# Encoder with two mixers: the last layer's second MLP product in three sweeps of seven block products, with weight sums made in DRAM

## The chip, the core and the metric

The kernel runs on one core of one Trainium2 chip. The core has five engines that run side by side and meet at semaphores: TensorE (PE; its weight loads are listed as PEld), VectorE (DVE), ScalarE (ACT), GpSimd (POOL) and SyncE (SP), which only starts transfers. ScalarE and GpSimd can start transfers too; 16 DMA engines carry them out. Each engine takes its instructions in the order of its queue. The time is the device time of one execution in microseconds; lower is better.

## The reference: what is computed

Two layers over 512 tokens (a grid of 8 x 64) of width 1024, all in float32. Layer 0 mixes with grouped-query attention and latent attention side by side, layer 1 with attention over a neighbourhood. Behind each stands an MLP with a squared ReLU, of hidden width 4096, and at the end an RMS norm.

```python
def sq_relu_mlp(h, w_up, w_down):
    u = jax.nn.relu(h @ w_up)
    return (u * u) @ w_down
...
        h = h + sq_relu_mlp(rmsnorm(h, norm_ffn[layer]), ffn_w_up[layer], ffn_w_down[layer])
    return rmsnorm(h, final_norm)
```

## The kernel before

The residual stays in SBUF as `hT`, features on partitions, 8 tiles of 128 features by 512 tokens. Every factor is split into a high part (written as float32r by ScalarE, `whi`) and a remainder (by VectorE, `wlo`), and every product is three matmuls: high by high, high by remainder, remainder by high. Weights come through a list of planned chunks: `plan` notes a chunk, `weights(i)` starts loads up to five chunks ahead and conversions two ahead. Large tiles are 30 slots of 128 x 1024 (`Slot`).

**The opening.** x and the first 768 columns of `w_in` are loaded in pieces by SP. For each of 8 feature tiles TensorE transposes x (`make_x`, L540), ScalarE and VectorE split it (L544, L545), and six output tiles are summed (`use_w`, L501 to L503). ScalarE squares each tile (`sumsq_acc`, L515) and POOL adds the squares up (L517) into `acc`; TensorE turns `acc` into row norms (`compact_r`, L522). Then come the statistics of key and queries (`stat`): ScalarE squares, VectorE rounds (L594), POOL makes the remainder (L595), TensorE sums both (L596, L597). The rotary products are POOL's too (L562, L563). `q_scales` gives the factor by which the scores of the first attention are scaled (L1001).

**The first attention** (`attend`) goes through 16 heads in four steps each, `step` being called once per step to run other products in between (`fill`).

**The MLPs** (`mlp(l)`). The first product makes hidden tiles, in groups (`SIZES`); most of it uses `Seven`, a scheme with seven instead of eight products of half-size blocks, whose weight sums POOL makes (`seven_chunk`, L302 to L304) and whose matmuls have 256 columns (L388 to L390). The second product for layer 1 takes 6, 8 and 6 of the 32 hidden tiles in plain form (`product`, matmuls of 512 columns), then 8 tiles in the `Seven` form, for which `convert` makes token sums and splits (L336 to L340, L362, L363), and the last 4 tiles with tokens on partitions (`last`, `down`), where the result meets the transposed residual (`turn`), the final norm and the output's transfers. `evac` (L1295) and `ev` (L1265) add to `hT`.

**What sets the order.** Outside the second attention (`fixed_order`) a scheduler places the instructions: it lets an engine take any instruction whose inputs are there, with the program's order as a preference, not as a rule. A transfer that depends on nothing can thus stand far ahead of its place in the text. Transfers share a small number of semaphores in turn, so that a new transfer may have to wait until an older one with the same semaphore has landed.

Of the kernel before, what the change touches and what calls it, by code (L numbers as in the profile page):

```python
# [8 lines left out]
F32 = mybir.dt.float32  # L9
# [26 lines left out]
def encoder_kernel(ctx: ExitStack, tc: tile.TileContext, ins, out, dbg=None):  # L36
# [736 lines left out]
    rope_q(0)  # L773


    kst = Slot()

    def ev_kr(b):
# [316 lines left out]
    attend(all_heads(), step)  # L1095
    fill.until("out")
    ok = [s_.pair() for s_ in O[4:]]
    flip[0] = 1
# [11 lines left out]
    def first_product(l):  # L1110

        w = ins["ffn_w_up"][l]
        X = [Slot() for _ in range(KD)]
        acc = pp.tile([P, S], F32, tag="p", name=nm("acc"))
        for k in range(KD):
            split_g(hT[:, k, :], gffn(l, k), X[k].pair())
            sumsq_acc(k, acc, DVE)
        xp = [s_.pair() for s_ in X]
        U, R = [], []
        rb = keep([P, S], F32, "rb")  # L1120
        state = dict(c=SIZES[l][0], ids=None, plain=False, split=iter(()))
# [24 lines left out]

        def raw_evac(w_):
            ACT.activation(w_.t, w_.t, AF.Relu)
            ACT.activation(w_.t, w_.t, AF.Square)
            R.append(w_)  # L1150
            return True

        def pair_evac(w_):
            raw_evac(w_)
            R.pop()
            for z in range(2):
                U.append(Slot())
                split(w_.t[:, S * z : S * z + S], U[-1].pair())

        def plain():  # L1160
            four = product(w, 0, xp, tiles(0, 512), ev, lambda n: [mmb(), mmb(), mmb(), sbk()])
            two = product(w, 0, xp, tiles(512, 256), ev, lambda n: [sbk(), ob()], kstep=4)
            for n, _ in enumerate(four):
                if n == (11 if l == 0 else 13):
                    norm()
                if n == 14:
                    x_sums(0)
                    x_sums(1)
            for n, _ in enumerate(two):
# [20 lines left out]
        def stage(n, raw=0, more=0):  # L1190

            if not state["plain"]:
                plain()
            left = n + raw + more - len(U)
            while left:
                i = state["ids"]
                state["c"] += 2
                left -= 2
                if left:
                    ahead()  # L1200
                for _ in x7.run(i, raw_evac if more <= left < more + raw else pair_evac):
# [12 lines left out]

    def bias_rows():
        R, Fi, Fe = Slot(F32), Slot(F32), Slot(F32)
        rpb = ins["od_rpb"][0]
        for qr in range(8):
            SP.dma_start(R.t[16 * qr : 16 * qr + 16, 0:248],
                           rpb.rearrange("h a b -> h (a b)")[:, (7 - qr) * 31 : (7 - qr) * 31 + 248])  # L1220
            yield
        POOL.memset(Fi.t[:, 0:376], NEG)
        POOL.memset(Fe.t[:, 256:512], NEG)
        rv = R.t[:, 0:248].rearrange("p (k d) -> p d k", d=31)
        POOL.tensor_copy(Fi.t[:, 0:376].rearrange("p (j k) -> p j k", k=8)[:, 15:31, :], rv[:, 7:23, :])
        POOL.tensor_copy(Fe.t[:, 0:248].rearrange("p (j k) -> p j k", k=8), rv)
        for _ in range(6):
            yield
        bxv = bx.rearrange("h t (c r) k -> t c r h k", r=8)
        for c in range(16):  # L1230
            SP.dma_start(bxv[0, c].rearrange("r h k -> r h k"), Fi.t[:, (15 - c) * 8 : (15 - c) * 8 + 256])
            yield

            v, off = (1, (7 - c) * 8) if c < 8 else (0, (23 - c) * 8)
            SP.dma_start(bxv[1, c][:, :, 128 * v : 128 * v + 128], Fe.t[:, off : off + 128])
            yield
            SP.dma_start(bxv[1, c][:, :, 128 - 128 * v : 256 - 128 * v], Fe.t[:, 256:384])
            yield
        for s_ in (R, Fi, Fe):
            s_.free()  # L1240
        yield

    def convert(u7, R):
        held = tc.keep_in_program_order
# [332 lines left out]
    def last_mlp():  # L1577
# [43 lines left out]
        def down(k0, c, up, tail):  # L1621

            nk = len(up)
            ids = [plan([(0, S, rows(ins["ffn_w_down"][1], k0 + k, 2)[:, :, S * c : S * c + S])], 2, S)
                   for k in range(0, nk, 2)]

            def run():
                banks = group(4)

                def use(k, j):  # L1630
                    wh, wl = (x[:, k % 2, :] for x in weights(ids[k // 2]))
                    uh, ul = (up[k][:, z, j * P : (j + 1) * P] for z in range(2))
# [22 lines left out]
        def last(k0, tiles_):  # L1655
# [4 lines left out]
            def beside(m, i):  # L1660
                if m == 2 and i == 0:
# [3 lines left out]
                if m > 1 and i in (16, 22):  # L1665
                    turn(2 * (m - 2) + (i == 22), 0)
# [62 lines left out]
```

## Time and profile before

| | us |
|---|---|
| median of 3 runs (1182.7 to 1184.34) | 1183.78 |
| the profiled execution: span | 1184.0 |
| first matmul of a score (L997) | 68.95 |
| row norms' matmuls (L522): first attention | 40.6 |
| the same, first MLP | 276.4 |
| the same, second attention | 613.3 |
| the same, last MLP | 838.1 |

The norms' matmuls mark the stages: what is called the opening here are the first 69 us, the last MLP is what runs from about 838 us to the end. A row of the windows gives a stretch's length, the busy time of PE, PEld, DVE, ACT and POOL with counts, TensorE's granted clock, the share of the 16 DMA engines and GB/s. A row of the timeline gives start, duration, engine, line, operation, result and inputs, and in brackets how long the engine had been idle and who ended that. A row of the waits gives who waited for whom: total, times, longest.

### The profile page before, as it was taken

What the parts mean: (1) busy time and instruction counts of PE and PEld (TensorE: products, weight loads), DVE (VectorE), ACT (ScalarE), POOL (GpSimd) and SP (SyncE); (2) the same over time, 40 slices, a digit from 0 to 9 for tenths busy, and PEclk for the clock granted to TensorE, in tenths of its full rate; (3) what the DMA queues carried; (4) which work ended last, traced back from release to release, by engine and by line L of the source; (5) the groups of instructions that cost most, each with busy time, mean ns of one, the idle gap of its engine ahead of it and who ended that gap; (6) DMA issues with size and microseconds to landing.
All of it is one profiled execution on the core that took longest, in us unless ns stands there. A gap on an engine that the chain in (4) does not pass through costs nothing.

```text
span 1184.0 us, 19784 instructions
## 1 busy us (share of the span) xinstructions
PE 1160.5 (98%) x7128; PEld 1021.2 (86%) x7128; DVE 883.2 (75%) x1514; ACT 640.3 (54%) x1081; POOL 526.1 (44%) x662
## 2 busy tenths in 40 slices
PE   9989999999999999999999999999999999999997
PEld 8667778888899899988998998988889989998895
DVE  5788998878967368786884676667996736778975
ACT  4468676664546247562553565555554624666344
POOL 3267343224562377819602232231376625774710
PEclk9999999999999999999999999999999999999998
DMA  7223225212524723225226464433352341322412
GB/s 244 71 54 92 68 78 134 62 56 77 167 86 134 263 70 90 72 90 165 67 72 178 131 184 126 116 112 109 107 165 76 115 134 55 98 64 89 143 36 71
DMA packets 110145, 128.01 MB, mean 108 GB/s; under 512 B 9075, under 2 KB 86816, under 8 KB 110048
## 3 DMA queue, kind: packets, MB, share of 16 engines
q1 hardware_dynamic: 106992, 119.30, 33.5%
q0 software_dynamic: 2304, 6.31, 2.2%
q8 instruction: 56, 0.92, 0.3%
q10 hardware_dynamic: 752, 1.15, 0.3%
q14 instruction: 41, 0.34, 0.1%
HBM read 104.32 MB, written 6.29 MB: 93 GB/s over the span
## 4 chain that ended last, share of the span: by engine, by line
PE 81%; DVE 4%; ACT 1%; issue 1%; POOL 0%; DVEq 0%; ACTq 0%
PE mm L503 8%; PE mm L501 8%; PE mm L502 8%; PE mm L390 4%; PE mm L389 4%; PE mm L388 4%; PE t L388 3%; PE t L389 3%; PE t L390 3%; PE s L502 2%; PE s L503 2%; PE s L501 2%; PE s L390 2%; PE s L388 2%; PE s L389 2%; PE s L997 2%
## 5 line engine op out<-in xcount | busy, mean ns | idle before, releaser
L309 DVE TENSOR_TENSOR wlo<-a,whi 128x896 fp32r<-128x896 f32 x132 | 161.8, 1230 | 83.7 <-ACT whi L308 82.9
L308 ACT ACTIVATE whi<-a 128x896 fp32r<-128x896 f32 x132 | 125.0, 950 | 155.0 <-PE o L502 45.8
L501 PE MATMUL mm<-a,whi 128*128 128x512 f32 x485 | 195.9, 406 | 0.9 <-DVE a L915 0.7
L503 PE MATMUL mm<-a,wlo 128*128 128x512 f32 x485 | 192.1, 397 | 2.5 <-DVE wlo L202 2.5
L502 PE MATMUL mm<-a,whi 128*128 128x512 f32 x485 | 192.5, 397 | 0.1
L202 DVE TENSOR_TENSOR wlo<-raw,whi 128x1024 fp32r<-128x1024 f32 (+4 forms) x117 | 139.3, 1193 | 66.4 <-ACT whi L212 63.9
L212 ACT ACTIVATE whi<-raw 128x1024 fp32r<-128x1024 f32 (+3 forms) x120 | 116.4, 971 | 92.2 <-PE s L502 39.8
L302 POOL TENSOR_TENSOR a<-a 128x128 f32<-128x128 f32 x132 | 85.1, 645 | 173.3 <-DMA a<-in_ffn_w_up_dram 103.9
L303 POOL TENSOR_TENSOR a<-a 128x256 f32<-128x256 f32 x132 | 120.2, 910 | 10.3
L304 POOL TENSOR_TENSOR a<-a 128x128 f32<-128x128 f32 x132 | 115.1, 872 | 10.3
L503 PEld LDWEIGHTS mm<-a,wlo 128*128 128x128 f32 x485 | 91.7, 189 | 23.7 <-DVE wlo L202 3.4
L501 PEld LDWEIGHTS mm<-a,whi 128*128 128x128 f32 x485 | 91.8, 189 | 20.4 <-PE t L972 0.9
L502 PEld LDWEIGHTS mm<-a,whi 128*128 128x128 f32 x485 | 91.9, 190 | 17.4 <-DVE a L545 0.4
L388 PE MATMUL mm<-a,whi 128*128 128x256 f32 x370 | 103.9, 281 | 0.0
L389 PE MATMUL mm<-a,whi 128*128 128x256 f32 x370 | 103.9, 281 | 0.0
L390 PE MATMUL mm<-a,wlo 128*128 128x256 f32 x370 | 103.7, 280 | 0.0
L1005 POOL TENSOR_SCALAR p<-p,ti 128x512 f32<-128x512 f32 x64 | 46.2, 724 | 92.3 <-DVE ti L1004 81.1
L1430 POOL TENSOR_SCALAR p<-p,ti 128x256 f32<-128x256 f32 x64 | 35.6, 567 | 104.8 <-DVE ti L1429 91.8
L388 PE MATMUL t<-a,whi 128*128 128x256 f32 x264 | 74.2, 281 | 0.0
L389 PE MATMUL t<-a,whi 128*128 128x256 f32 x264 | 74.1, 281 | 0.0
L390 PE MATMUL t<-a,wlo 128*128 128x256 f32 x264 | 73.9, 280 | 0.0
L390 PEld LDWEIGHTS mm<-a,wlo 128*128 128x128 f32 x370 | 69.6, 188 | 0.2 <-DVE wlo L309 0.2
(338 smaller groups left out, 3210.8 us busy)
## 6 DMA issues: line engine op xcount, KB each, us to landing
a<-in_ffn_w_up_dram SPq DMA_DIRECT2D x104, 256.0 KB
raw<-in_ffn_w_down_dram SPq DMA_DIRECT2D x46, 512.0 KB
raw<-in_od_w_qkv_dram SPq DMA_DIRECT2D x64, 128.0 KB
a<-in_ffn_w_down_dram SPq DMA_DIRECT2D x28, 256.0 KB
raw<-in_ffn_w_up_dram SPq DMA_DIRECT2D x12, 512.0 KB
raw<-in_ev_w_in_dram SPq DMA_DIRECT2D x12, 384.0 KB
a<-a SPq DMA_DIRECT2D x18, 256.0 KB
bias<-bx SPq DMA_DIRECT2D x16, 256.0 KB
```

The costliest lines, as they stand in the source:

```text
L202: z = lambda: (eng or DVE).tensor_tensor(to, src, f32(high), op=ALU.subtract)
L212: ACT.activation(hi[:, 0:m], raw[:, 0:m], AF.Copy)
L303: POOL.tensor_tensor(r[:, 4:6], r[:, 2:3].to_broadcast([P, 2, P]), r[:, 0:7:6], op=ALU.add)
L304: POOL.tensor_tensor(r[:, 7], r[:, 3], r[:, 5], op=ALU.subtract)
L308: ACT.activation(hi[:, 0:896], raw[:, 128:1024], AF.Copy)
L309: DVE.tensor_tensor(lo[:, 0:896], raw[:, 128:1024], f32(hi[:, 0:896]), op=ALU.subtract)
L388: PE.matmul(o, wh, x[:, 0], start=kp == 0 and n in (0, 1, 3, 5), stop=False, skip_group_check=True)
L389: PE.matmul(o, wh, x[:, 1], start=False, stop=False, skip_group_check=True)
L390: PE.matmul(o, wl, x[:, 0], start=False, stop=kp == self.np - 1, skip_group_check=True)
L501: PE.matmul(o, wh, xh, start=first, stop=False)
L502: PE.matmul(o, wh, xl, start=False, stop=False)
L503: PE.matmul(o, wl, xh, start=False, stop=last)
```

## The change

In layer 1, `mlp_swept` takes the place of `mlp`. Six hidden tiles go through the plain product as before. The next 22 stay in float32 (11 slots `R`, each with two tiles) and the second product over them is made in three sweeps over all 11 pairs (`Sweeps`): two, two and three of the seven block products, each for four output tiles at once, in six PSUM banks. Token sums are made in place on VectorE just ahead of each step and split into a slot. Weight operands are blocks of the weights or sums of blocks, all with plus signs. The sums aren't made on POOL when a chunk is loaded, but once, in DRAM (`SumsAhead`): ScalarE's queue copies the 11 pairs of weight rows (1 MB each) to a DRAM tile `made`, and POOL's queue starts four adding DMAs of 256 KB for each pair. The program asks for one of them in each step of the first attention from the fifth on. The transposes `turn(j, 0)` move into `down`.

```diff
+    class SumsAhead:
+        def __init__(self, w, k0, n):
+            self.w, self.k0, self.n = w, k0, n
+            self.made = dr.tile([n, 2, P, 1024], F32, name=nm("made"))
...
+        def steps(self):
+            for kp in range(self.n + 4):
+                if kp < self.n:
+                    k = self.k0 + 2 * kp
+                    ACT.dma_start(self.made[kp].rearrange("z p c -> (z p) c"), self.w[k * P : (k + 2) * P, :])
+                for back, z, f, src in ((2, 1, 1, lambda q: self.weight(q, 0, 1)), (2, 0, 1, lambda q: self.weight(q, 0, 0)),
+                                        (3, 0, 0, lambda q: self.block(q, 1, 1)), (4, 1, 0, lambda q: self.block(q, 0, 0))):
+                    if 0 <= kp - back < self.n:
+                        POOL.dma_start(self.block(kp - back, z, f), src(kp - back), accum_op=ALU.add)
+                        yield
...
+        if n > 3:
+            next(sums1, None)
         fill.run(1.5)
 
+    ahead1 = SumsAhead(ins["ffn_w_down"][1], FIRST, RAW // 2)
+    sums1 = ahead1.steps()
...
+    def sweep_chunk(w, k0, kind, made):
...
+        if kind == 0:
+            for z in range(2):
+                SP.dma_start(line(a[:, S * z : S * z + S]), half(k0 + z, 0))
+        else:
+            for z in range(2):
+                SP.dma_start(line(a[:, S * z : S * z + S]), blocks(made[z])[:, (z, 1 - z)[kind - 1]])
...
+        ACT.activation(hi, a, AF.Copy)
+        DVE.tensor_tensor(lo, a, f32(hi), op=ALU.subtract)
...
+            if kind == 0:
+                split_to(d[:, :, 0], d[:, :, 1], r[:, 0:4:2])
+                self.one(kp)
+                if kp < 2:
+                    self.two(kp)
+            elif kind == 1:
+                for q, src in enumerate((r[:, 0], s2)):
+                    split_to(d[:, q, 0], d[:, q, 1], src)
+                if kp + 2 < self.n:
+                    self.two(kp + 2)
...
+            PRODUCTS = [
+                [(X, 0, at(0)), (Z, 1, at(S))],
+                [(Y, 0, at(S)), (X, 1, at(0))],
+                [(Y, 2, at(S)), (Z, 1, lambda h, m: (h[2].t[:, 0:S], h[2].t[:, S:], P * m)), (X, 0, at(0))],
+            ]
...
+                PE.matmul(o, wh, x[:, 0], start=first and m % 2 == 0, stop=False, skip_group_check=True)
+                PE.matmul(o, wh, x[:, 1], start=False, stop=False, skip_group_check=True)
+                PE.matmul(o, wl, x[:, 0], start=False, stop=last, skip_group_check=True)
...
+                if c == 0:
+                    for j in range(4):
+                        turn(j, 0)
...
-        mlp(1, last)
+        mlp_swept(1, ahead1, last)
```

Where the new transfers stand in the built program. First POOL's queue at the very start, as a difference (`made` is the DRAM tile, `acc` the sum of squares, `sc` a scratch tile):

```order
 L130 DMA a_82<-in_final_norm_dram 8x128
+L806 DMA made_621<-in_ffn_w_down_dram 256x256 x4
+L806 DMA made_621<-made_621 256x256 x2
+L806 DMA made_621<-in_ffn_w_down_dram 256x256
 L517 ISA
 L517 TENSOR_TENSOR acc_122<-acc_122,sc_248 128x512
+L806 DMA made_621<-in_ffn_w_down_dram 256x256
 L517 TENSOR_TENSOR acc_122<-acc_122,sc_283 128x512
+L806 DMA made_621<-made_621 256x256
```

Seven adding DMAs now stand ahead of POOL's first addition of squares, and more between the next ones. Second, POOL's queue at the remainders of the key's and the first query tile's statistics (L595), with the semaphores each instruction waits for (DMAHW: a transfer from SP or ScalarE; DMASW: one from POOL). Before:

```order
L517 TENSOR_TENSOR acc_122<-acc_122,sc_384 128x512 [waits Activation_49,Pool_49]
L595 TENSOR_TENSOR sc_434<-sc_432,sc_433 128x512 [waits DVE_49]
L562 TENSOR_TENSOR sc_475<-sc_440,a_132 128x512 [waits PE_49,DMAHW7_49,Activation_49,Pool_49]
L595 TENSOR_TENSOR sc_524<-sc_522,sc_523 128x512 [waits DVE_49,PE_49]
L595 TENSOR_TENSOR sc_539<-sc_537,sc_538 128x512 [waits DVE_49,Pool_49]
```

And in the change, the end of that stretch:

```order
L806 DMA made_621<-made_621 256x256 [waits DMASW7_49,DMASW4_49]
L806 DMA made_621<-in_ffn_w_down_dram 256x256 [waits DMAHW6_49]
L806 DMA made_621<-in_ffn_w_down_dram 256x256 [waits DMASW6_49]
L806 DMA made_621<-made_621 256x256 [waits DMASW1_49]
L806 DMA made_621<-made_621 256x256 [waits DMASW3_49,DMASW0_49]
L806 DMA made_621<-made_621 256x256 [waits DMASW5_49]
L595 TENSOR_TENSOR sc_524<-sc_522,sc_523 128x512 [waits DVE_49,PE_49]
```

Ahead of this L595 stand 42 of the 44 adding DMAs (30 of them ahead of the key's L595); the wait for DMAHW6 in the second row is the one for the last of the 11 copies. Third, ScalarE's queue in the opening, in the change (`whi`: weight casts; `a_114`, `a_115`: tiles of x; before, the same casts and tiles stand there without the L802 rows):

```order
L140 ACTIVATE ti_109<-zeros 128x1 [waits Pool_49]
L802 DMA made_621<-in_ffn_w_down_dram 16x16384
L802 DMA made_621<-in_ffn_w_down_dram 16x16384 [waits DMAHW0_49]
L143 ACTIVATE gT<-t_111 128x16 [waits PE_49]
L212 ACTIVATE whi_150<-raw_148 128x768 [waits DMAHW6_49]
L544 ACTIVATE a_114<-t_155,gT 128x512 [waits PE_49,Activation_49]
L544 ACTIVATE a_115<-t_167,gT 128x512 [waits PE_49]
L802 DMA made_621<-in_ffn_w_down_dram 16x16384 [waits DMAHW3_49]
L212 ACTIVATE whi_177<-raw_175 128x768 [waits DMAHW1_49]
```

Two copies are started before the first tile of x is scaled, and all 11 before the seventh (`a_120`).

More of the change, by code (lines that the diff above doesn't have):

```diff
@@ L1095, in encoder_kernel @@
     attend(all_heads(), step)
+    assert next(sums1, 0) == 0
     fill.until("out")
@@ L1120, in first_product @@
         rb = keep([P, S], F32, "rb")
-        state = dict(c=SIZES[l][0], ids=None, plain=False, split=iter(()))
+        state = dict(c=FIRST, ids=None, plain=False, split=iter(()))
         x7 = Seven(KD)
@@ L1188, in ahead, with stage @@
             state["ids"] = x7.plan(w, P * state["c"])
-        def stage(n, raw=0, more=0):
+        def stage(n, raw=0, more=0, then=lambda: None):
             if not state["plain"]:
@@ L1200, in stage @@
                     ahead()
+                else:
+                    then()
                 for _ in x7.run(i, raw_evac if more <= left < more + raw else pair_evac):
@@ L1241, in bias_rows, with raw, half @@
         yield
+    def sweep_chunk(w, k0, kind, made):
+        def raw():
+            slot = Slot(F32) if len(free) > reserve[0] else None
+            return slot, slot.t if slot else wp.tile([P, 1024], F32, tag="raw", bufs=4, name=nm("raw"))
+        def half(k, f):
+            return w[k * P : (k + 1) * P, :].rearrange("p (z f n) -> p f z n", z=2, f=2)[:, f]
+        sa, a = raw()
+        sb, b = raw() if kind == 2 else (None, None)
+        if kind == 0:
+            for z in range(2):
+                SP.dma_start(line(a[:, S * z : S * z + S]), half(k0 + z, 0))
+        else:
+            for z in range(2):
+                SP.dma_start(line(a[:, S * z : S * z + S]), blocks(made[z])[:, (z, 1 - z)[kind - 1]])
+        if kind == 2:
+            SP.dma_start(line(b[:, 0:S]), half(k0 + 1, 1))
+        yield
+        hi = wp.tile([P, 1024], F32R, tag="whi", name=nm("whi"))
+        lo = wp.tile([P, 1024], F32R, tag="wlo", name=nm("wlo"))
+        ACT.activation(hi, a, AF.Copy)
+        DVE.tensor_tensor(lo, a, f32(hi), op=ALU.subtract)
+        third = None
+        if kind == 2:
+            third = Slot()
+            ACT.activation(third.t[:, 0:S], b[:, 0:S], AF.Copy)
+            DVE.tensor_tensor(third.t[:, S:], b[:, 0:S], f32(third.t[:, 0:S]), op=ALU.subtract)
+        for s_ in (sa, sb):
+            if s_:
+                s_.free()
+        yield (hi, lo, third), None, []
@@ new lines, in mlp_swept, with ev, split_more @@
+    def mlp_swept(l, made, last):
+        stage, ahead, later = first_product(l)
+        w = ins["ffn_w_down"][l]
+        U = stage(FIRST)[0]
+        up = [s_.pair() for s_ in U]
+        def ev(m, b):
+            DVE.tensor_tensor(hT[:, m, :], hT[:, m, :], b, op=ALU.add)
+        gens = [product(w, 0, up, tiles(512 * c, 512), lambda j, b, c=c: ev(4 * c + j, b)) for c in range(2)]
+        ahead()
+        for c, gen in enumerate(gens):
+            for i, _ in enumerate(gen):
+                later(c, i)
+        for s_ in U:
+            s_.free()
+        reserve[0] = 3
+        sweeps = []
+        R = stage(0, RAW + MORE, 0, lambda: sweeps.append(Sweeps(w, FIRST, made)))[1]
+        R, more = R[: RAW // 2], R[RAW // 2 :]
+        V = [Slot() for _ in range(MORE)]
+        def split_more():
+            for n, v in enumerate(V):
+                raw = more[n // 2]
+                split(raw.t[:, S * (n % 2) : S * (n % 2) + S], v.pair())
+                if n % 2:
+                    raw.free()
+                yield
+        rest = split_more()
+        reserve[0] = 6
+        beside = last(FIRST + RAW, V)
+        for n, (kind, kp) in enumerate(sweeps[0].run(R)):
+            beside(kind, kp)
+            if n % 16 == 15:
+                next(rest, None)
+        assert next(rest, 0) == 0
+        reserve[0] = 1
@@ L1658, in last, with beside @@
             runs.extend(down(k0, c, up, 2 + 2 * c) for c in range(2))
-            def beside(m, i):
-                if m == 2 and i == 0:
+            def beside(kind, kp):
+                if (kind, kp) == (2, 6) and not H:
                     H.extend(Slot(F32) for _ in range(4))
@@ L1664, in beside @@
                     SP.dma_start(G[0].t, ins["final_norm"].unsqueeze(0).to_broadcast([P, D]))
[L1665 to L1670 removed]
+            return beside
+        mlp_swept(1, ahead1, last)
+        flip[0] = 1
         for run in runs:
```

131 lines of the change are left out of this document (added).

## The prediction

> **What bounds the kernel now.** I read the page's busy table and its slices first, to see whether one engine sets the time.
>
> ```profile
> span 1184.0 us, 19784 instructions
> PE 1160.5 (98%) x7128; PEld 1021.2 (86%) x7128; DVE 883.2 (75%) x1514; ACT 640.3 (54%) x1081; POOL 526.1 (44%) x662
> PE   9989999999999999999999999999999999999997
> PE 81%; DVE 4%; ACT 1%; issue 1%; POOL 0%; DVEq 0%; ACTq 0%
> ```
>
> TensorE is busy for 98% and makes up 81% of the chain that ended last; POOL is nowhere on that chain. So the time is TensorE's work plus its few gaps. The profiled execution's 1184.0 us agrees with the median of the runs, 1183.78 us, and I sum against 1184.0. A difference under 0.2%, about 2.4 us, is what a measurement of this kernel can't tell from no change.
>
> Next, the two places that the change touches. In the last MLP (from about 838 us) the waits of TensorE, and the timeline behind the one that matters:
>
> ```profile
> PE mm L503 <- DVE wlo L202: 2.2, 1, 2.2
> 1102.58 0.79 PE L503 MATMUL mm<-a,wlo 128*128 128x512 f32 x1 [2.23 <-DVE wlo L202]
> 1103.17 0.63 PE L501 MATMUL mm<-a,whi 128*128 128x512 f32 x1
> ...
> 1106.56 0.40 PE L501 MATMUL mm<-a,whi 128*128 128x512 f32 x1
> ```
>
> TensorE waits there once, 2.23 us, while VectorE converts the raw tiles for the old seven-product part. Behind it nine matmuls take 3.39 us instead of nine times 0.232: another 1.3 us.
>
> The opening, by windows (columns: length; busy time of PE, weight load, DVE, ACT and POOL with counts; granted clock; DMA share; GB/s):
>
> ```profile
> 0.00:54.00 54.00, 51.79 (x251) 42.32 (x252) 32.02 (x70) 24.23 (x37) 14.28 (x22) 1.00 0.50 163
> 10.00:15.00 5.00, 5.00 (x26) 4.11 (x25) 3.42 (x6) 3.28 (x5) 1.52 (x1) 1.00 1.07 392
> 45.00:80.00 35.00, 28.56 (x117) 19.78 (x116) 28.56 (x75) 18.30 (x34) 14.32 (x11) 0.95 0.23 62
> ```
>
> TensorE is full nearly from the start, and the transfers of the first 54 us are 163 GB/s x 54 us = 8.8 MB. When the 16 DMA engines are full (share 1.07) they load 392 GB/s, that is 366 GB/s at a share of 1.
>
> POOL's place in the opening, from its timeline:
>
> ```profile
> 30.46 1.29 POOL L517 TENSOR_TENSOR acc<-acc,sc 128x512 f32<-128x512 f32 x1 [3.27 <-ACT sc L515]
> 40.67 1.27 POOL L595 TENSOR_TENSOR sc<-sc,sc 128x512 fp32r<-128x512 f32 x1 [8.92 <-DVE sc L594]
> 53.91 1.29 POOL L595 TENSOR_TENSOR sc<-sc,sc 128x512 fp32r<-128x512 f32 x1 [10.26 <-DVE sc L594]
> PE t L597 <- POOL sc L595: 1.4, 3, 0.8
> ```
>
> POOL idles for its inputs here, but TensorE waits for each of these results: L517's sum feeds the row norms (L522), L595's remainders feed the statistics of key and queries (L597), and without these no score is scaled. POOL's idleness is slack only as long as nothing that waits stands in front of these instructions.
>
> **The MLP, part by part.** Removed: 14 contraction tiles of plain second product, 8 tiles x 14 x 3 = 336 matmuls of 512 columns. Added: they join the seven-product part, so its block products go from 4 x 4 x 7 x 3 = 336 to 11 x 7 x 4 x 3 = 924 matmuls of 256 columns. TensorE's step, start to start, for the two kinds:
>
> ```profile
> 879.69 0.40 PE L501 MATMUL mm<-a,whi 128*128 128x512 f32 x1
> 881.78 0.40 PE L501 MATMUL s<-a,whi 128*128 128x512 f32 x1
> ...
> 1009.81 0.28 PE L390 MATMUL s<-a,wlo 128*128 128x256 f32 x1
> 1011.93 0.28 PE L390 MATMUL s<-a,wlo 128*128 128x256 f32 x1
> ```
>
> Between the first two lie 9 steps: 2.09/9 = 0.232 us. Between the other two lie 18: 2.12/18 = 0.118 us. So 336 x 0.232 = 78.0 us go, 588 x 0.118 = 69.3 us come: **8.7 us less**. The burst of conversions that caused the 2.23 us wait goes as well, since tokens are now converted one step ahead of each sweep step: 2.2 + 1.3 = 3.5 us. What is late next there is VectorE. It now does in each step of a sweep one weight remainder of 1024 columns, token remainders of 512 (768 and a weight remainder of 512 in the third sweep) and one or two sums of 256:
>
> ```profile
> L202 DVE TENSOR_TENSOR wlo<-raw,whi 128x1024 fp32r<-128x1024 f32 x8 | 10.1, 1263 | 7.6 <-ACT whi L212 7.6
> L363 DVE TENSOR_TENSOR a<-a,a 128x512 fp32r<-128x512 f32 x12 | 10.6, 925 | 0.7 <-ACT a L362 0.7
> L363 DVE TENSOR_TENSOR a<-a,a 128x256 fp32r<-128x256 f32 x4 | 1.9, 478 | 0.0
> L1265 DVE TENSOR_TENSOR hT<-hT,mm 128x512 f32<-128x512 f32 x3 | 1.9, 675 | 0.0
> L363 DVE TENSOR_TENSOR a<-a,a x68: 406/684/1231, 308.3 to 1105.0; 128x512 fp32r<-128x512 f32 x51, 128x256 fp32r<-128x256 f32 x17
> ```
>
> The first three rows, means of 1060 to 1150 us, are beside a busy POOL. With them the three sweeps' steps cost 1.26 + 0.93 + 0.48 = 2.67, 1.26 + 2 x 0.48 + 0.48 = 2.70 and 1.26 + 2 x 0.93 + 3 x 0.48 = 4.56 us, against TensorE's 24, 24 and 36 matmuls: 2.83, 2.83 and 4.25 us. Near its limit in the first two, above it in the third. But POOL no longer makes sums in this stage, and L363's median and minimum of one (684 and 406 ns) say what such pieces take undisturbed: 2.3, 2.5 and 3.9 us, below TensorE. I cost the sweeps at TensorE's time; if that cover is gone, eleven steps of the third sweep lose 0.3 us each and the 8 additions into the residual between the sweeps 0.68 us each (L1265): about 9 us. The weights' loads (512 KB in 2.83 us, 185 GB/s) are below the 392 of the window above. The transposes of the first half move from between the old products to between the last plain ones: same number, same cost. Sum of the MLP: 8.7 + 3.5 = **12.2 us less**.
>
> **The opening.** The code asks for one adding DMA per step of the first attention, but the built order, shown with the change, has all 11 copies and all 44 adding DMAs ahead of it: the copies between ScalarE's first activations, the additions between POOL's L517 and L595. Their issuing waits for the copy, or for an earlier addition, and POOL takes its queue in order. So the L595 that ran at 53.91 us now stands behind 42 additions, of which some 37 must have landed, and all 11 copies before them. Behind it stand POOL's other L595s and the rotary product, and on TensorE L597 and all that follows. ScalarE's copies also wait on DMAs, in front of its weight casts, and SP's fourth piece of x waits on the first copy; these waits end with the same bytes, so I don't count them again.
>
> The bytes that must move before that L595: 11 copies of 1.049 MB are 11.53 MB, 37 additions of 0.262 MB are 9.70 MB, and 8.8 MB that are loaded now. No row of this trace copies within DRAM or adds; the nearest are the load above and the writing of the output into DRAM at the end:
>
> ```profile
> 1178.00:1182.00 4.00, 0.00 (x0) 0.00 (x0) 0.98 (x3) 0.72 (x1) 0.00 (x0) 0.50 0.86 255
> a<-a POOLq DMA_DIRECT2D x16, 256.0 KB, 3.4
> ```
>
> 255 GB/s at a share of 0.86 is 297 GB/s for writing to DRAM. A copy ends with such a write, an addition reads two sources. **Low end:** every byte passes once at 392 GB/s: 30.0 MB / 392 = 76.6 us, plus 3.3 us until the first copy is issued, less 53.9: 26 us. **High end:** reads and writes each take their own time: copies 31.5 + 38.8, additions 53.0 + 32.7, loads 24.0, in all 180 us: 129 us later. **Taken:** a copy at the writing row, 11.53/297 = 38.8 us; an addition by its two reads, 2 x 9.70/366 = 53.0 us; loads 24.0 us. With 3.3 that is 119.2, which is 65.3 us after 53.9. The 3.4 us from issue to landing of a 256 KB POOL transfer does not bind: 44 of them, some four in flight, are 37 us. Below nothing the term can't come: POOL can't pass those waits earlier than now. TensorE has 6.4 us of idle time at 45 to 80 us (the window above) that may be taken up, and the slow clock behind three long waits costs 1.3 us or more each; I set these against each other.
>
> The Trainium skill speaks against this change ("DMA: Bandwidth & Descriptors", Issuing engines are not separate DMA queues): transfers started by ScalarE, SP and GpSimd run on the same 16 DMA engines. The share of 1.07 says no more than that these are full at 392 GB/s; that three queues don't add to it no row here shows. The same page (Latency and other measured facts) gives 207 to 214 GB/s for copies between DRAM tensors; by that the copies would take 55 us instead of 38.8, and the sum would be 16 us more, about 1253 us.
>
> **The sum:** 1184.0 - 12.2 + 65.3 = **1237 us**.
>
> **The rivals.**
> - The transfers hide, and only the MLP's part is left: 1184.0 - 12.2 = 1172 us. For it: the DMA share is 0.50 in the first 54 us, and POOL is busy for 14 of 54. Against it: 30.0 MB in 53.9 - 3.3 = 50.6 us are 593 GB/s, one and a half times the fullest row. The change pays from 30.0/(50.6 + 12.2) = 478 GB/s on.
> - The queues drain faster than the writing row says, at the fullest load's rate or a little over: 20 to 30 us held, 1184.0 - 12.2 + 25 = 1197 us.
> - VectorE does not keep up in the sweeps and the MLP gains some 3 us: 1246 us, on top of a held opening. POOL's silence speaks against it, the narrow margin of the third sweep for it.
> - The additions are slower than reads and writes apart: over 1301 us. Nothing here shows how fast a DMA engine adds.
>
> **How the numbers follow.** The opening held by 30 to 129 us: 0.78, most likely 65. Held by less, still slower: 0.08. Hidden: 0.06. About even: 0.02. Beyond 129 us: 0.06. The sweeps bound by VectorE, 0.2 of any of these, moves the time by 9 us only. The range reaches from 1190, which is an opening held by 18 us and takes in half of the second rival, to the high end, 1184.0 - 12.2 + 129 = 1301: it leaves out 0.06 + 0.02 + 0.04 below and 0.06 above. Faster: 0.06, same 0.02, slower 0.92.
>
> **What would show it.** Right: the DMA share near 1 from about 5 us until far past 54, the L595 of the first query tile starting near 119 us, TensorE idle in front of L522 and L597, slices of POOL empty but for DMA issue; behind that the same kernel, shifted; in the last MLP 924 matmuls at 0.118 us and no wait for L202. Wrong: L595 near 54 us (then the copies are cheap), a wait for VectorE's token remainders in each third-sweep step, or a wait of TensorE for weights from the DRAM sums.

## The result: slower by 54 us

| kernel | median us | runs | lowest to highest | against the kernel before: ratio, 95% interval |
|---|---|---|---|---|
| before, on the same chip | 1184.06 | 4 | 1182.70 to 1185.06 | |
| the change | 1238.21 | 4 | 1235.99 to 1239.32 | 1.0453, 1.0439 to 1.0468 |

Against a prediction of 1237 us, the kernel takes 1238.2. First the page after: busy times, then three rows of slices (TensorE's busy time, its granted clock, the share of the DMA engines), and the chain by engine:

```profile
span 1234.2 us, 20486 instructions
PE 1167.0 (95%) x7380; PEld 1036.1 (84%) x7380; DVE 892.0 (72%) x1565; ACT 656.6 (53%) x1116; POOL 524.2 (42%) x658
PE   6736999999999999999999999999999999999997
PEclk8857999999999999999999999999999999999999
DMA  9999233151234265232432556433334323366702
PE 83%; DMA 8%; DVE 4%; issue 1%; POOL 1%; ACT 1%; SPq 0%; DVEq 0%; ACTq 0%; POOLq 0%
```

TensorE loses more time than before in the first four slices (one is 31 us) and nowhere else, and there the share of the DMA engines is 0.9 or more. Transfers, which were not on the chain before, are 8% of it. The last norm's matmuls (L522; the last number of the range of starts) divide the loss from the gain. Before, then after:

```profile
L522 PE MATMUL t<-ones,acc x32: 164/250/250, 40.6 to 838.6; 128*128 128x1 f32 x32
```

```profile
L522 PE MATMUL t<-ones,acc x32: 164/250/352, 91.4 to 900.8; 128*128 128x1 f32 x32
```

Everything up to the last MLP came 900.8 - 838.6 = **62.2 us later**. From there to the end it took 1184.0 - 838.6 = 345.4 us before and 1234.2 - 900.8 = 333.4 after: **12.0 us less**.

What TensorE waited for, all of the change's waits over 2 us (who for whom: total, times, longest):

```profile
PE mm L502 <- DVE a L545: 20.9, 4, 19.6
PE mm L501 <- ACT a L544: 15.2, 3, 8.4
PE t L597 <- POOL sc L595: 9.6, 3, 7.1
PE t L755 <- issue: 3.3, 1, 3.3
```

All of them are in the opening; together they are 49.0 us. The largest group are not the norms or the statistics but the tiles of x, whose high part is made by ScalarE (L544) and whose remainder by VectorE (L545). ScalarE was late because pieces of `w_in` were: in front of its casts (L212) it waited in the first 140 us for

```profile
ACT whi L212 <- DMA raw<-in_ev_w_in_dram: 35.8, 7, 10.2
```

and in the kernel before for 1.1 us. VectorE's timeline in front of the longest wait, and then the matmul that waited:

```profile
85.46 0.69 DVE L517 TENSOR_TENSOR acc<-acc,sc 128x512 f32<-128x512 f32 x1 [22.64 <-POOL acc L517]
...
87.03 0.75 DVE L545 SCALAR_TENSOR_TENSOR a<-t,gT,a 128x512 fp32r<-128x512 f32 x1
```

```profile
87.83 0.80 PE L502 MATMUL mm<-a,whi 128*128 128x512 f32 x1 [19.64 <-DVE a L545]
```

VectorE stood for 22.64 us in front of the sixth addition to the sum of squares, because GpSimd's fifth had not been made; the last tile of x was queued behind it. Why GpSimd was late stands on the chain (start, length):

```profile
42.12 1.16 POOL acc L517
43.33 0.58 POOL made L806
43.91 27.82 DMA made<-in_ffn_w_down_dram
71.73 0.28 issue
72.02 8.93 DMA made<-made
```

An addition issued at 43.91 landed at 71.73, and a later one waited for it at the head of GpSimd's queue, where GpSimd itself was idle for 11.15 us. Behind that one stood seven more additions, and the fifth L517 ran at 83.14:

```profile
72.02 0.88 POOL L806 DMA_DIRECT2D made<-made  x1 [11.15 <-DMA made<-in_ffn_w_down_dram]
...
83.14 2.28 POOL L517 TENSOR_TENSOR acc<-acc,sc 128x512 f32<-128x512 f32 x1
...
93.50 1.95 POOL L595 TENSOR_TENSOR sc<-sc,sc 128x512 fp32r<-128x512 f32 x1
...
114.49 1.59 POOL L595 TENSOR_TENSOR sc<-sc,sc 128x512 fp32r<-128x512 f32 x1
```

The last row is the first query tile's, 53.91 before. Three stretches of the windows, two in the opening, one in the sweeps:

```profile
5.00:10.00 5.00, 2.19 (x18) 1.88 (x17) 1.52 (x2) 0.18 (x1) 0.77 (x2) 1.00 1.22 455
70.00:120.00 50.00, 23.50 (x80) 17.08 (x81) 20.77 (x54) 10.20 (x19) 30.08 (x32) 0.66 1.19 201
1100.00:1150.00 50.00, 50.00 (x427) 50.00 (x426) 50.00 (x93) 29.14 (x48) 0.00 (x0) 1.00 0.63 197
```

While copies and loads fill the engines they move 455 GB/s; while mostly additions do, 201 GB/s at nearly the same share (1.22 and 1.19). An addition's bytes are counted once in this, as a copy's are. TensorE works 23.5 of those 50 us, at a granted clock of 0.66, so the opening pays in slower matmuls too: up to the first score TensorE is busy for 59.9 us before (5 to 69 us, 284 matmuls, clock 1.00) and for 77.3 after (5 to 132.8 us, 279 matmuls, clock 0.75), 17.4 us more for the same work. In the sweeps TensorE and VectorE are both busy all the time and TensorE waits for nothing.

### The profile page after: what moved, and what is told of

Same layout as the page of the kernel before. It is cut to its first block, busy times and chain, and to the rows that moved or that the text cites. A ratio compares the mean times of both kernels' runs of the same rounds, so it can differ in the third digit from the quotient of the medians.

```text
span 1234.2 us, 20486 instructions
## 1 busy us (share of the span) xinstructions
PE 1167.0 (95%) x7380; PEld 1036.1 (84%) x7380; DVE 892.0 (72%) x1565; ACT 656.6 (53%) x1116; POOL 524.2 (42%) x658
## 4 chain that ended last, share of the span: by engine, by line
PE 83%; DMA 8%; DVE 4%; issue 1%; POOL 1%; ACT 1%; SPq 0%; DVEq 0%; ACTq 0%; POOLq 0%
PE mm L501 7%; PE mm L503 7%; PE mm L502 7%; PE mm L390 3%; PE mm L389 3%; PE mm L388 3%; DMA made<-made 3%; PE s L1030 2%; DMA made<-in_ffn_w_down_dram 2%; PE o L1018 2%; PE t L388 2%; PE t L389 2%; PE t L390 2%; DMA raw<-in_ev_w_in_dram 2%; PE s L502 2%; PE s L503 2%
## 5 line engine op out<-in xcount | busy, mean ns | idle before, releaser
L502 PE MATMUL mm<-a,whi 128*128 128x512 f32 x443 | 179.9, 406 | 20.9 <-DVE a L545 20.9
L501 PE MATMUL mm<-a,whi 128*128 128x512 f32 x443 | 182.5, 415 | 16.2 <-ACT a L544 15.2
L309 DVE TENSOR_TENSOR wlo<-a,whi 128x896 fp32r<-128x896 f32 x116 | 144.3, 1247 | 68.5 <-ACT whi L308 67.5
L202 DVE TENSOR_TENSOR wlo<-raw,whi 128x1024 fp32r<-128x1024 f32 (+4 forms) x103 | 121.8, 1185 | 79.9 <-ACT whi L212 77.4
L308 ACT ACTIVATE whi<-a 128x896 fp32r<-128x896 f32 x116 | 109.8, 949 | 130.1 <-PE o L502 36.7
L503 PE MATMUL mm<-a,wlo 128*128 128x512 f32 x443 | 178.6, 404 | 0.0
L212 ACT ACTIVATE whi<-raw 128x1024 fp32r<-128x1024 f32 (+3 forms) x106 | 101.4, 959 | 120.8 <-DMA raw<-in_ev_w_in_dram 35.8
L502 PEld LDWEIGHTS mm<-a,whi 128*128 128x128 f32 x443 | 86.1, 194 | 39.0 <-DVE a L545 22.7
L302 POOL TENSOR_TENSOR a<-a 128x128 f32<-128x128 f32 x116 | 73.5, 633 | 99.1 <-DMA a<-in_ffn_w_up_dram 64.8
L304 POOL TENSOR_TENSOR a<-a 128x128 f32<-128x128 f32 x116 | 98.4, 849 | 9.1
L503 PEld LDWEIGHTS mm<-a,wlo 128*128 128x128 f32 x443 | 85.8, 194 | 19.4 <-issue 0.6
L389 PE MATMUL mm<-a,whi 128*128 128x256 f32 x330 | 92.7, 281 | 0.0
L388 PE MATMUL mm<-a,whi 128*128 128x256 f32 x330 | 92.5, 280 | 0.0
L1038 POOL TENSOR_SCALAR p<-p,ti 128x512 f32<-128x512 f32 x64 | 48.5, 760 | 86.4 <-DVE ti L1037 77.0
L389 PE MATMUL t<-a,whi 128*128 128x256 f32 x232 | 65.1, 281 | 0.0
L388 PE MATMUL t<-a,whi 128*128 128x256 f32 x232 | 65.1, 280 | 0.0
L390 PEld LDWEIGHTS mm<-a,wlo 128*128 128x128 f32 x330 | 62.1, 188 | 0.5 <-DVE wlo L309 0.5
```

The source lines that it names most:

```text
L202: z = lambda: (eng or DVE).tensor_tensor(to, src, f32(high), op=ALU.subtract)
L212: ACT.activation(hi[:, 0:m], raw[:, 0:m], AF.Copy)
L304: POOL.tensor_tensor(r[:, 7], r[:, 3], r[:, 5], op=ALU.subtract)
L308: ACT.activation(hi[:, 0:896], raw[:, 128:1024], AF.Copy)
L309: DVE.tensor_tensor(lo[:, 0:896], raw[:, 128:1024], f32(hi[:, 0:896]), op=ALU.subtract)
L388: PE.matmul(o, wh, x[:, 0], start=kp == 0 and n in (0, 1, 3, 5), stop=False, skip_group_check=True)
```

## The experiments

Each row below is one kernel; the kernel before ran on the same chip as each group (medians 1183.99, 1183.58 and 1183.46 us). Differences between groups carry the half microsecond by which these differ. "Last L522" is the latest start of that line in the profile, against 838.6 before.

| kernel | median us | ratio to before, 95% interval | last L522 |
|---|---|---|---|
| sweeps alone | 1171.97 | 0.9902, 0.9882 to 0.9923 | 836.4 |
| sums alone | 1248.89 | 1.0541, 1.0512 to 1.0569 | 902.3 |
| copies, no additions | 1186.67 | 1.0023, 1.0008 to 1.0038 | 848.4 |
| additions an eighth as long | 1198.13 | 1.0116, 1.0092 to 1.0140 | 864.0 |
| plain copies for the additions | 1214.51 | 1.0254, 1.0230 to 1.0278 | 880.5 |
| 22 of the 44 additions | 1218.35 | 1.0286, 1.0263 to 1.0309 | 883.2 |
| VectorE for GpSimd in the opening | 1229.40 | 1.0380, 1.0356 to 1.0404 | 892.9 |
| sums in the first attention | 1219.06 | 1.0298, 1.0275 to 1.0321 | 882.1 |
| sums in the first MLP | 1199.75 | 1.0126, 1.0100 to 1.0152 | 866.0 |
| sums in the second attention | 1193.80 | 1.0085, 1.0059 to 1.0112 | 858.0 |
| **sums spread** | **1176.93** | **0.9939, 0.9916 to 0.9962** | 840.5 |

### Both halves of the change by themselves

Sweeps alone: no copies, no additions, and the sweeps read blocks of the weights where they would read sums (same shapes and bytes; the sums are left out).

```diff
-        if n > 3:
-            next(sums1, None)
...
-        mlp_swept(1, ahead1, last)
+        mlp_swept(1, RAW // 2, last)
```

> The three sweeps without any transfer in the opening: the copies and the adding DMAs are left out, and the sweeps read blocks of the weights in place of the sums, so that loads and matmuls are the same and the values of the last product are not. Theory A (two parts that add up: the last MLP gives 12 us, the opening takes 62): 1184 - 12 = 1172 us, with the first L595 of the query tiles back at 54 us. Rival C (the parts depend on each other, or a part of the 62 us comes from another order of instructions): the time is more than 3 us away from 1172.

Sums alone: the kernel before, with the copies and additions put in and nothing that reads them.

```diff
+        if n > 3:
+            next(sums1, None)
...
+    ahead1 = SumsAhead(ins["ffn_w_down"][1], FIRST, RAW // 2)
+    sums1 = ahead1.steps()
```

> The kernel before with the copies and the adding DMAs of the change, whose result nothing reads. Theory A: the opening is held as in the change, 1184 + 62 = 1246 us, and the last MLP takes the 345 us of before. Rival C: less than 1240 or more than 1252.

1171.97 and 1248.89: the sweeps are worth 12.0 us, the sums cost 64.9, and 1183.99 - 12.0 + 64.9 = 1236.9 is the change within its spread. Both are as their theories A said, and beyond some 1.3 us the two do not touch each other.

### What of the sums costs the time

Copies without additions (the sums are left out: `made` holds plain weights).

```diff
-                        POOL.dma_start(self.block(kp - back, z, f), src(kp - back), accum_op=ALU.add)
+                        pass
```

> The change without its 44 adding DMAs (the sums are left out, the sweeps read copied weights); the 11 copies stay where they are. Theory A (the hold is the sum of all bytes in front of L595; additions had 76 us of the queue's packet time in the change, copies 32): 11.5 MB of copies and 8.8 MB of loads are 56 us behind 3.3, so L595 of the first query tile at some 60 us instead of 54, and 1184 - 12 + 6 = 1178 us, 1184 if copies go at the rate of the output's writing. Rival B (TensorE's first and longest waits in the change are on tiles of x, L544 and L545, whose loads stand with the copies in the queues, so the copies hold it and the additions matter little): at least 36 us of the hold stay, 1208 us or more.

1186.67 is just above theory A (1178 to 1184) and far from rival B; the first query tile's L595 starts at 65.83 us, where 60 was expected. The copies cost 14.7 us over the sweeps alone, the additions the other 1238.2 - 1186.7 = 51.5. The one long wait that the copies make (this kernel's waits):

```profile
PE t L540 <- DMA a<-in_x_dram: 6.0, 1, 6.0
```

It is a piece of x: a load that the copies hold up. Next, three cuts in the 51.5 us. Plain copies of the same blocks:

```diff
-                        POOL.dma_start(self.block(kp - back, z, f), src(kp - back), accum_op=ALU.add)
+                        POOL.dma_start(self.block(kp - back, z, f), src(kp - back))
```

> The change with the 44 additions turned into plain copies of the same blocks (same queue, same 1 KB rows, same order of waits; the sums are left out, so the values are not the reference's). Theory A (the rows and the queue are the price, the adding is free): as the change, 1230 to 1240. Theory B (the adding is the price: what is added to must be read too): between the copies alone (1187) and the change, 1190 to 1212.

Half of the additions:

```diff
-                    if 0 <= kp - back < self.n:
+                    if back == 2 and 0 <= kp - back < self.n:
```

> The change with the 22 additions of weight blocks alone; the 22 that add a made block to another are left out, so the values are not the reference's. Theory A (a price for each addition, 51.6 us over 44, or 1.17 each above the copies alone): 1187 + 26 = 1213, from 1207 to 1219. Theory B (the chain is the price: a made block waits for the one before to land, 8 to 9 us each time, on GpSimd's queue): under 1200.

All additions, on 16 of each block's 128 rows:

```diff
+                        POOL.dma_start(self.block(kp - back, z, f)[0:16], src(kp - back)[0:16], accum_op=ALU.add)
```

> The change with each of the 44 additions cut to 16 of its 128 rows of a block: the same number of issues, the same chain and the same waits at the head of GpSimd's queue, an eighth of the rows and bytes (the sums are therefore not complete). Theory A (the rows on the DMA engines are the price): 1187 + 51.6 / 8 = 1193, from 1187 to 1200. Theory B (GpSimd's queue is the price: 44 issues of about 1 us and the waits for a landing of several us each): 1212 to 1235.

Above the copies' 1186.67 they cost 27.8, 31.7 and 11.5 us. The first is a little above its theory B and far below A: as plain copies the blocks cost about half, so the adding, with its longer issues and three times the packets, is the other 23.7. The second is on the side of a price for each addition (1.44 us for each of the 22, where 1.17 was expected), not of the chain, which this kernel does not have. The third is in theory A's range (1187 to 1200): with the same 44 issues and the same chain, seven eighths of the rows gone took 40 of the 51.5 us away. So **the rows are most of the price**. Where they cost it, on the DMA engines or in GpSimd's queue, this kernel does not part: shorter additions land sooner (after 5.1 us in place of 8.5, medians), so the waits at the head of the queue are not the same, though its expectation says so. For landings, in front of its issues, GpSimd was idle in the change (us, times):

```profile
DMA made<-in_ffn_w_down_dram: 41.4, 7
DMA made<-made: 16.3, 8
```

and with an eighth of the rows:

```profile
DMA made<-in_ffn_w_down_dram: 13.4, 6
DMA made<-made: 9.3, 2
```

That is 57.7 and 22.7 us. The 11.5 us that are left are the most that the 44 issues can cost by themselves; they say nothing of the waits that went with the rows.

The page's third part shows what an addition is to the engines (queue, packets, MB, share of 16 engines' span). GpSimd's queue (q0) and ScalarE's (q10) before:

```profile
q0 software_dynamic: 2304, 6.31, 2.2%
q10 hardware_dynamic: 752, 1.15, 0.3%
```

after:

```profile
q0 software_dynamic: 14272, 17.85, 8.3%
q10 hardware_dynamic: 1104, 12.69, 2.6%
```

and with plain copies of the blocks:

```profile
q0 software_dynamic: 5824, 17.85, 5.3%
```

The 44 additions are 11,968 packets of about 1 KB, and 8.3% x 1234.2 - 2.2% x 1184.0 = 76 us of all 16 engines, 11.53 MB / 76 = 151 GB/s. The same blocks copied are 3,520 packets and 5.3% x 1213.8 - 26.0 = 38 us. The 11 large copies are 32.1 - 3.6 = 28.5 us, 405 GB/s. (In the windows the share passes 1, up to 1.22, so packets lie over each other, and these are rates of the packets, not by the clock.)

### GpSimd's queue

VectorE does the opening's sums of squares, cosine products and remainders:

```diff
-        POOL.tensor_tensor(c[0:n, :], src[0:n, :], cos[0:n, :], op=ALU.mult)
+        DVE.tensor_tensor(c[0:n, :], src[0:n, :], cos[0:n, :], op=ALU.mult)
...
-        POOL.tensor_tensor(lo, sq, f32(hi), op=ALU.subtract)
+        DVE.tensor_tensor(lo, sq, f32(hi), op=ALU.subtract)
...
-        sumsq_acc(k, acc)
+        sumsq_acc(k, acc, DVE)
```

> The change, with GpSimd's arithmetic of the opening (the squares' sums L517 for x tiles 1 to 5, the cosine products L562, the remainders L595) done by VectorE, so that none of it is queued behind the additions. Theory A (the DMA engines are the bound: the weights of the opening, the last of which ScalarE received at 40 us, and the additions hold it whatever GpSimd does): 1225 to 1240. Theory B (GpSimd's queue is the bound: it stood 27.8 us in front of an addition, and the fifth L517 and VectorE's queue behind it): the copies' hold stays, the 47 us go mostly: 1187 to 1205.

1229.4, so 8.8 us less than the change, within theory A by the time. It doesn't part the theories, for a new wait took the old ones' place:

```profile
PE mm L503 <- POOL wlo L202: 22.5, 1, 22.5
```

L202 on GpSimd is a weight's remainder that I had left there, and it too was queued behind the additions: it ran at 124.67 us. What was taken off GpSimd did come sooner, the first row norms at 73.8 us in place of 91.4, the first query tile's L595 at 87.25 in place of 114.49. So GpSimd's queue did hold the opening, and how much of the 51.5 us is left without it stays open: a kernel with nothing at all on GpSimd in the opening was not tried. (The expectation misreads two rows of the change: the 27.8 us are a transfer's way to its landing, of which GpSimd stood 11.15, and ScalarE's last long wait for `w_in` ended at 52.45 us, not at 40.)

### Other places for the same sums

In the first attention, where the code asks for them (each transfer held behind what was traced before it):

```diff
-                    ACT.dma_start(self.made[kp].rearrange("z p c -> (z p) c"), self.w[k * P : (k + 2) * P, :])
+                    tc.keep_in_program_order(ACT.dma_start(self.made[kp].rearrange("z p c -> (z p) c"), self.w[k * P : (k + 2) * P, :]))
...
-                        POOL.dma_start(self.block(kp - back, z, f), src(kp - back), accum_op=ALU.add)
+                        tc.keep_in_program_order(POOL.dma_start(self.block(kp - back, z, f), src(kp - back), accum_op=ALU.add))
```

> The change with each copy and each adding DMA pinned behind the instruction that precedes it on its engine in the program's text, so that they stand in the first attention, one addition to a step. Theory A: the opening is as before and the MLP's 12 us remain; POOL has 44 issues of 0.6 to 0.9 us more in an attention in which it is 80% busy at 80 to 120 us, which may cost up to 10 us: 1172 to 1182, most likely 1175. Rival D (an addition costs where it stands, since POOL waits for older ones, some 8 us from issue to landing, in front of the normalised scores that TensorE needs): over 1195 us, with TensorE waiting for L1038 in the attention.

1219.06, still 47 us over the sweeps alone, though L595 is back near its place (40.3 us for the first of them). That is rival D by the time, but not by the wait that it named: L1038 is not among TensorE's waits. The timeline of TensorE at the longest wait, and the window around it:

```profile
102.22 0.76 PE L1030 MATMUL s<-a,a 128*128 128x512 f32 x1 [16.41 <-DMA a<-sc]
```

```profile
80.00:100.00 20.00, 5.81 (x34) 4.37 (x33) 6.45 (x17) 5.61 (x13) 8.17 (x11) 0.70 0.90 262
```

A score waits for the last of the rotation's three moves between partitions (128 KB each). The first was issued at 83.0 us, among four copies of 1 MB that were started from 81 to 85 us, the third only at 96.1; in the sweeps alone all three are issued from 80.7 to 82.9. The attention has small transfers on its path; the opening has loads on its path. I took the first MLP to have neither, so the same pinned transfers went there, one addition at every sixth step of its second products:

```diff
+                    one_sum()
...
+    def one_sum():
+        turns[0] += 1
+        if turns[0] % 6 == 0:
+            next(sums1, None)
```

> The change with the 11 copies and 44 additions held in the second product of the first MLP, one addition at every sixth step, instead of the first attention. Theory A (the sums cost time only where something short or early hangs on a transfer: the opening's loads, the rotary shuffles; in the MLP before, the DMA engines' share is 0.26 to 0.59 and no TensorE wait stands in 290 to 480 us): the time of the sweeps alone, 1172, up to 1178. Theory B (the additions cost their 47 us wherever they stand, as they did in the pinned attention): 1215 to 1222. Theory C (GpSimd's weight sums L302 to L304 fall behind the additions' landings and the passes wait for them): 1185 to 1205, with TensorE waits on L308 or L309.

1199.75, in theory C's range. Waits and one window of this kernel:

```profile
PE s L388 <- ACT whi L308: 9.2, 3, 8.4
PE s L501 <- ACT whi L212: 4.2, 1, 4.2
```

```profile
580.00:620.00 40.00, 32.18 (x253) 31.89 (x254) 30.29 (x31) 18.59 (x25) 32.80 (x37) 0.87 0.82 147
```

The longest wait, 8.4 us, is theory C's: the chain goes from an addition that took 10.05 us to land (from 574.46) to L304, queued behind it on GpSimd (585.88), and to ScalarE's L308. The wait for L212 is not: ScalarE had stood there for the transfers of the bias rows (`bx`, 64 or 128 KB each), 24.5 us in two waits, so small transfers are on the path here too. The additions did not come one by one: 18 were issued from 296 to 407 us, where the MLP also writes the bias rows, none in the next 107 us, and 26 from 515 to 617 us, where the window shows TensorE at work for 32 of 40 us. Next, all in the second attention, three before each head:

```diff
+        if n:
+            for _ in range(3):
+                next(sums1, None)
```

> All copies and additions in the second attention, three before each head from the second on. Theory A (there is room: TensorE waited there for nothing over 0.2 us without the sums, and the DMA share was 0.36 to 0.65): 1172 to 1183. Theory B (as in the first attention, where they cost 47 us): 1200 to 1222, with TensorE waits for VectorE or DMA in the second attention.

1193.8, between the two theories. Two waits and a window:

```profile
PE s L1695 <- DMA a<-sc: 9.3, 2, 6.9
PE mm L1655 <- DVE sc L1598: 7.1, 1, 7.1
```

```profile
680.00:720.00 40.00, 33.14 (x187) 29.32 (x187) 23.08 (x61) 18.23 (x43) 20.20 (x30) 0.89 1.15 276
```

Again a small move waits where the engines are full. Last, thinly over both: every fourteenth step of the first MLP without its middle third, and two before each head of the second attention.

```diff
+                    if z != 1:
+                        one_sum()
...
+        if turns[0] % 14 == 0:
+            next(sums1, None)
...
+        if n:
+            for _ in range(2):
+                next(sums1, None)
```

> The copies and additions spread thinly: one addition at every fourteenth step of the first MLP's second products except the middle third, in which the bias rows are written (18 additions), and the other 26 in the second attention, two before each head. Theory A (what the sums cost is the work that they hold up where they bunch; thinly laid they are hidden): 1172 to 1183, that is, at or below the kernel before. Theory B (they hold up small transfers wherever those are, the second attention's moves between partitions too): 1190 to 1215, with TensorE waits on L1030's likes in the second attention.

**1176.93 us: below both, and in theory A's range**; it is 6.5 us less than the kernel before, a ratio of 0.9939. Where its additions are issued, and its two fullest windows:

```profile
L806 POOL DMA_DIRECT2D made<-in_ffn_w_down_dram x22: 859/888/1553, 299.6 to 756.8; - x22
L806 POOL DMA_DIRECT2D made<-made x22: 871/984/1282, 502.0 to 780.8; - x22
```

```profile
660.00:700.00 40.00, 40.00 (x251) 35.65 (x251) 27.21 (x76) 23.00 (x55) 18.33 (x30) 1.00 0.98 243
700.00:740.00 40.00, 40.00 (x266) 36.43 (x265) 26.28 (x74) 23.60 (x57) 18.44 (x30) 1.00 0.96 228
```

All the bytes and packets are still moved (9.1% on q0), the share reaches 0.98, and TensorE is busy 40 of 40 us. Its last L522 is at 840.5, 4.1 us after the sweeps alone: of the 62 to 66 us that the same sums cost in the opening, some 5 are left. The additions do not come evenly here either: 3 from 300 to 319 us, 15 from 501 to 594, 26 from 650 to 781. In the second attention the place is the same as in the kernel above and only the number differs: with 44 additions in 166 us TensorE worked 66 of the 80 us from 640 to 720, with 26 in 131 us all 80.

## Why the prediction was right, step by step

- **The MLP, 12.2 us less: right.** 12.0 by the profiles, 12.0 by the sweeps alone. The matmul counts and the wait for L202 behaved as said; no TensorE wait stands behind 900.8 us.
- **The sweeps' cover on VectorE: right, and as narrow as said.** I costed its steps at 2.3, 2.5 and 3.9 us against TensorE's 2.83, 2.83 and 4.25. The groups from 1100 to 1166 us (count, busy us, mean ns):

```profile
L1306 DVE TENSOR_TENSOR wlo<-a,whi 128x1024 fp32r<-128x1024 f32 x18 | 22.4, 1252 | 0.2 <-ACT whi L1305 0.2
L1354 DVE TENSOR_TENSOR a<-a,a 128x512 fp32r<-128x512 f32 x13 | 8.8, 710 | 0.1
L1354 DVE TENSOR_TENSOR a<-a,a 128x256 fp32r<-128x256 f32 x22 | 8.6, 447 | 0.0
L1344 DVE TENSOR_TENSOR a<-a,a 128x256 f32<-128x256 f32 x11 | 5.1, 462 | 0.0
L1340 DVE TENSOR_TENSOR a<-a 128x256 f32<-128x256 f32 x11 | 5.1, 461 | 0.0
L1311 DVE TENSOR_TENSOR a<-raw,a 128x512 fp32r<-128x512 f32 x7 | 5.0, 735 | 0.0
...
L1336 DVE SCALAR_TENSOR_TENSOR a<-a 128x256 f32<-128x256 f32 x9 | 3.8, 444 | 0.0
```

  With sums of 256 at 0.44 to 0.46 us that is 1.25 + 0.71 + 0.44 = 2.4, 1.25 + 2 x 0.45 + 0.44 = 2.6 and 1.25 + 0.74 + 0.71 + 0.45 + 2 x 0.46 = 4.1 us. The median of single instructions was the better guide than the means taken beside a busy GpSimd; that rival falls.
- **The opening, 65.3 us more: right in size.** 62.2 by the profiles, 64.9 for the sums alone. The L595 that was to start near 119 us started at 114.49.
- **Its two terms were each off, in opposite directions.** All 11 copies were to take 38.8 us at the output's 297 GB/s: their packets took 28.5. All 44 additions were to take 11.53 x 2 / 366 = 63.0 us by their two reads: theirs took 76. The sums, 101.8 and 105, agree by luck as much as by reason. By the clock, 30.6 MB were moved from 3.3 us to that L595 (275 GB/s for 111.2 us), where I had counted 30.0. What the kernel pays is a third thing: 14.7 us for the copies, of which part hides, and 51.5 for the additions.
- **Two things that I let go for nothing were not small.** From issue to landing I took 3.4 us for an addition and let it not bind; it took 8.5 (median), and GpSimd stood for 57.7 us in front of issues. And I set the slow clock, "1.3 us or more" for each of three waits, against 6.4 us of idle time; the slower matmuls came to 17.4 us. The first score starts 63.9 us later: 46.4 more of idle TensorE and these 17.4.
- **The Trainium skill's rate for copies, 207 to 214 GB/s** ("DMA: Bandwidth & Descriptors", Latency and other measured facts) would, as an estimate, have made it 1253, 15 us more than the kernel takes. The Trainium skill states it for tiles with rows of 16 KiB at two row pitches; here, in rows of 64 KB, the copies' packets moved 405 GB/s (of packet time), so the measurement decides against it for this layout. The other rule of that page of the Trainium skill (Issuing engines are not separate DMA queues), that transfers started by these three engines run on the same 16 DMA engines, fits: ScalarE waited 35.8 us for loads from SP's queue with its own and GpSimd's transfers under way, and 1.1 us before.
- **Where TensorE waits was named wrongly.** I had put the whole hold on GpSimd's order and looked for idle time in front of L522 and L597. L597 has 9.6 us, L522 none; 36.1 us stand in front of the tiles of x (L544, L545). I had seen the loads and ScalarE's casts behind the copies and let them go as the same bytes. They are the same bytes, which may be why the sum holds (no run shows that), but they made TensorE stop earlier, and VectorE's queue behind GpSimd's L517 added a way that I had not traced. It matters for a remedy: taking the named instructions off GpSimd gave back 8.8 us of 62, for another stood behind them in the same queue.
- **The rival in which all hides** (1172 us) was rejected for this place, rightly. The spread kernel shows that it was rejected for the place alone.

## What to carry to other kernels

A transfer that nobody waits for still has a price, set by what is under way around it: the same 11 copies and 44 additions cost 66, 47, 28, 22 or 5 us (medians over the sweeps alone) in the opening, the first attention, the first MLP, the second attention, or spread over the last two. Find where they really stand, since a scheduler may hoist what the code asks for late; then look for small transfers and first loads on the path, and lay the bulk thinly. In the second attention thinness decided: with 26 of the additions TensorE was busy all through 80 us in which it had lost 14 with all 44. Cost such a transfer by its packets too, not by its bytes alone.

## What was unexpected of the hardware

- An adding DMA of 256 KB in rows of 1 KB took twice the packet time of a plain copy of the same block (76 and 38 us for 44) and over three times the packets (11,968 and 3,520).
- Its issue keeps GpSimd longer. After, and with plain copies (durations in ns: shortest, median, longest):

```profile
L806 POOL DMA_DIRECT2D made<-made x22: 872/878/1916, 18.7 to 120.6; - x22
```

```profile
L806 POOL DMA_DIRECT2D made<-made x22: 557/557/581, 16.7 to 100.0; - x22
```

- Engines at nearly the same share (1.22 and 1.19) moved 455 GB/s in one window and 201 in another: the share says that they are occupied, not how much they move.
